# Sixteen more chunks of a decoder layer as seven products, with local attention, head and tail rearranged

## The chip, the cores and the metric

One core of one Trainium2 chip runs the whole layer. The metric is the device time of one execution in microseconds (us). Three runs of the kernel before gave a median of 2082.5 us (2082.36 to 2082.59).

## The reference

A decoder layer on 256 tokens of width 2048, all in float32. Every `w` is a weight in HBM; a mixer has eight channel groups that mix tokens (u, v) beside a sliding-window attention of 16 heads (q, k, v), and a cross-attention of four heads reads 256 rows of memory.

```python
h = x
h = h + 0.5 * swiglu(rmsnorm(h, g_ffn1), w1_gate, w1_up, w1_down)   # 2048 -> 5632 -> 2048
z = rmsnorm(h, g_mix) @ w_in                                        # u, v, q, and a narrow k, v
y_a = spatial_gating(z[..., :o_q], g_v, w_s, b_s)                   # gelu(u) * (w_s @ norm(gelu(v)) + b_s)
y_b = window_attention_sinks(q, k, v, sinks)
h = h + concat(rmsnorm(y_a), rmsnorm(y_b)) @ w_out
h = h + cross_attention(rmsnorm(h, g_x), rmsnorm(mem, g_mem), w_xq, w_xkv, w_xo)
h = h + 0.5 * swiglu(rmsnorm(h, g_ffn2), w2_gate, w2_up, w2_down)
return rmsnorm(h, g_final)
```

## The kernel before

**Numbers.** Float32 factors are split into a high part (a cast to the rounded type fp32r, L150, on ACT) and a low part (a subtraction, L151, on DVE). A product of two such factors is three passes on PE: high by high, high by low, low by high.

**Chunks.** The tokens stand as two blocks of 128. Weights come from HBM in chunks of 1 MB, [128, 4, 512]: four slots, two row groups by two column groups, which is a 2 x 2 block of a matrix (B11, B12, B21, B22). `load` (L303) issues the DMA on SP's queue, and splits the chunk into `wh` and `wl`; there are three `raw` buffers and two of `wh` and of `wl`. A chunk meets a *pair* of rows of the activations, also 2 x 2 (A11 to A22, with their own high and low parts). `Unit.multiply` (L354) multiplies it in one of three kinds:

- N and C: four sums of two products, 8 x 3 passes = 24 matmuls of 512 columns. C gathers them so that a later S chunk can add to the same banks.
- S: seven products instead of eight (Strassen's scheme, in Winograd's form), 7 x 3 = 21 matmuls. They need four sums of weight slots, `t` (L314, L317, L318, on DVE), split into `th` and `tl` (one buffer each), sums of rows of the pair (L198 to L208), and at the end of the unit sums of the seven results (`seven_early`, `seven_late`, L496 to L511).

A *unit* is a series of chunks that adds up in the same four to eight PSUM banks. Four banks are accumulators of the pool `acc`; four more, of the pool `trp`, hold the other results (P1, Q6, Q7, R) and everything small: transposes and attention.

**Stages.** In this order: f1g (11 units of 8 chunks, gate and up of the first FFN), f1d (22 pairs by two halves of w_down, in four units of 8, 15, 14 and 7 chunks), q, a narrow kv, v, u, mv and mk (values and keys of the memory), wo (out of the mixer), xq (memory queries, two units), xo, f2g, f2d. The kinds of a unit's chunks are written as a string. f1g and f2g have `KINDS` = "CCSCSCSC", mv1 and mk `KINDS_M`, the down stages `KINDS_D` (a kind for each of the 22 pairs), whose six S stand for 12 S chunks in each FFN. q, v, u, mv0 and xq are plain: `unit` (L446) with eight N chunks. Altogether 102 chunks are of kind S.

**Order.** PE runs in the order of the program (`PINNED`). The other engines' instructions are put in order by a scheduler. `push` loads a chunk and leaves its multiplication pending until the next `push` has issued its own load, so that DVE and ACT are one chunk ahead of PE. After every sixth matmul `side_step` runs a piece of side work (transposes, attention, normalization), except in chunks that the unit marks `alone`, and in a run of S chunks whose banks are the `trp` ones. `post` of a unit's last chunk reads its results, in high priority; `later` holds work that is done some pushes on.

**Head.** `prep1` and `plain_gu_unit` run the first f1g unit in kind N: 12 warm-up matmuls (L99) on a tile of ones, the first chunk's weights in four pieces, the transposed input xT in [128, 2, 256] blocks (the first on ACT's queue, L86), and from chunk 1 the blocks of x for `h`. Rows are scaled and split straight from xT (`split_scaled`), and the rows of other units are normalized and transposed beside it.

**Tail.** `ffn` for f2 adds to `h` (L537); `on_final` takes squares of each 512 columns (L140, ACT) and the product with the final gain (L1263). After the last matmul: `rstd_of` for both token blocks (a sum, a multiply-add, a power on POOL, L129 to L135), then the scaling by it (L1277, L1282, L1285) and the output DMAs.

**Local attention.** `attend` (L925) is a side generator. In each round it writes scores `sc`, takes the softmax, transposes the probabilities `pT`, and multiplies them by the values into `po`, one `trp` bank that it holds for all its rounds.

## Time and profile before

| what | kernel before |
|---|---|
| median of three runs | 2082.5 us |
| the profiled execution | 2082.59 us |
| its span in the profile | 2080.9 us |
| PE, matmuls in flight | 2065.4 us (99%), 9518 instructions |
| PE, weight loads | 1712.7 us (82%) |
| DVE busy | 1684.6 us (81%), 1621 instructions |
| ACT busy | 1137.1 us (55%), 1104 instructions |
| DMA | 402.16 MB, 193 GB/s on average |

The profiled execution's own time is 1.7 us longer than its span. Matmuls overlap, so that an instruction's duration (0.39 us for 512 columns) is longer than the distance to the next one's start. A DVE instruction's duration, too, reaches a little beyond the start of the next one.

### The profile page before, as it was taken

To read this page: it belongs to the slowest core of one execution; us is meant where nothing else is said; L and a number is where in the kernel's file an instruction comes from. 1 tells how busy PE (TensorE), PEld (TensorE's weight loads), DVE (VectorE), ACT (ScalarE), POOL (GpSimd) and SP (SyncE) were. 2 spreads that over 40 slices of the span, in tenths; PEclk is the share of its full clock that TensorE was granted. 3 is DMA by queue.
4 is the path that set the end of the run, shared out by engine and by line. 5 is a ranking of instruction groups with operands and counts; after the bars stand their busy time and mean duration, and the time that the engine had idled before them with its cause. 6 is when DMAs were issued, how large, how long until landed. Compare 5 with 4: busy or idle time off the path is not lost.

```text
span 2080.9 us, 23813 instructions
## 1 busy us (share of the span) xinstructions
PE 2065.4 (99%) x9518; PEld 1712.7 (82%) x9518; DVE 1684.6 (81%) x1621; ACT 1137.1 (55%) x1104; POOL 30.2 (1%) x51
## 2 busy tenths in 40 slices
PE   9999999999999999999999999999999999999998
PEld 7788888888888888888888888888888888888886
DVE  5988888888987845968888656798888888889877
ACT  7655555555544655555555455665555555555444
POOL 0000000000000000200000000000000000000000
PEclk9999999999999999999999999999999999999999
DMA  8555555555555564535555544455555555555563
GB/s 305 182 199 206 201 191 182 207 198 195 202 201 202 198 227 167 184 137 201 189 195 186 181 160 143 181 194 210 182 206 197 203 184 202 202 202 202 185 219 121
DMA packets 60111, 402.16 MB, mean 193 GB/s; under 512 B 6864, under 2 KB 8928, under 8 KB 12768
## 3 DMA queue, kind: packets, MB, share of 16 engines
q1 hardware_dynamic: 57280, 393.50, 52.7%
q0 software_dynamic: 2016, 6.30, 0.9%
q8 instruction: 74, 1.21, 0.2%
q10 hardware_dynamic: 704, 0.84, 0.1%
q14 instruction: 37, 0.30, 0.0%
HBM read 398.52 MB, written 2.10 MB: 193 GB/s over the span
## 4 chain that ended last, share of the span: by engine, by line
PE 97%; DVE 2%; ACT 1%; issue 0%; DMA 0%; POOLq 0%; POOL 0%; SPq 0%; DVEq 0%
PE f2gQ L368 16%; PE f1gQ L368 15%; PE f2dQ L368 6%; PE f1dQ L368 6%; PE f2gP L368 6%; PE f1gP L368 5%; PE f2dP L368 3%; PE f1dP L368 3%; PE woQ L368 2%; PE xoQ L368 2%; PE xqQ L368 2%; PE f2dR L368 2%; PE f1dR L368 2%; PE mk1Q L368 1%; PE mk0Q L368 1%; PE mv1Q L368 1%
## 5 line engine op out<-in xcount | busy, mean ns | idle before, releaser
L151 DVE TENSOR_TENSOR f1gwl<-f1gw,f1gwh 128x2048 fp32r<-128x2048 f32 (+1 forms) x91 | 185.7, 2042 | 55.8 <-ACT f1gwh L150 55.6
L150 ACT CAST f2gwh<-f2gw 128x1536 fp32r<-128x1536 f32 (+1 forms) x88 | 154.3, 1753 | 133.2 <-PE f2gQ L368 97.6
L150 ACT CAST f1gwh<-f1gw 128x2048 fp32r<-128x2048 f32 (+1 forms) x91 | 155.9, 1714 | 126.0 <-PE f1gQ L368 89.4
L151 DVE TENSOR_TENSOR f2gwl<-f2gw,f2gwh 128x1536 fp32r<-128x1536 f32 (+1 forms) x88 | 183.6, 2087 | 41.1 <-ACT f2gwh L150 40.9
L368 PE MATMUL f2gQ<-f2gwh,n4fh 128*128 128x512 f32 x363 | 141.4, 390 | 0.0
L368 PE MATMUL f2gQ<-f2gwh,n4fl 128*128 128x512 f32 x363 | 141.3, 389 | 0.0
L368 PE MATMUL f1gQ<-f1gwh,n1fh 128*128 128x512 f32 x330 | 128.8, 390 | 0.0
L368 PE MATMUL f1gQ<-f1gwh,n1fl 128*128 128x512 f32 x330 | 128.5, 389 | 0.0
L150 ACT CAST f1dwh<-f1dw 128x2048 fp32r<-128x2048 f32 (+1 forms) x44 | 79.1, 1797 | 84.5 <-PE f1dQ L368 65.3
L150 ACT CAST f2dwh<-f2dw 128x2048 fp32r<-128x2048 f32 (+1 forms) x44 | 79.1, 1797 | 83.3 <-PE f2dQ L368 67.8
L368 PE MATMUL f2gQ<-f2gwl,n4fh 128*128 128x512 f32 x363 | 115.7, 392 | 0.0
L151 DVE TENSOR_TENSOR f1dwl<-f1dw,f1dwh 128x2048 fp32r<-128x2048 f32 (+1 forms) x44 | 94.2, 2143 | 26.1 <-ACT f1dwh L150 23.5
L151 DVE TENSOR_TENSOR f2dwl<-f2dw,f2dwh 128x2048 fp32r<-128x2048 f32 (+1 forms) x44 | 94.2, 2143 | 22.8 <-ACT f2dwh L150 20.0
L368 PE MATMUL f1gQ<-f1gwl,n1fh 128*128 128x512 f32 x330 | 105.1, 392 | 0.0
L151 DVE TENSOR_TENSOR f2gtl<-f2gt,f2gth 128x2048 fp32r<-128x2048 f32 x33 | 75.6, 2291 | 17.9 <-ACT f2gth L150 17.4
L151 DVE TENSOR_TENSOR f1gtl<-f1gt,f1gth 128x2048 fp32r<-128x2048 f32 x30 | 68.7, 2291 | 16.7 <-ACT f1gth L150 16.2
L368 PEld LDWEIGHTS f2gQ<-f2gwh,n4fl 128*128 128x128 f32 x363 | 68.1, 188 | 14.2
L368 PEld LDWEIGHTS f2gQ<-f2gwh,n4fh 128*128 128x128 f32 x363 | 68.2, 188 | 14.1
L368 PEld LDWEIGHTS f2gQ<-f2gwl,n4fh 128*128 128x128 f32 x363 | 67.3, 188 | 13.5
L150 ACT CAST f2gth<-f2gt 128x2048 fp32r<-128x2048 f32 x33 | 63.1, 1912 | 24.8 <-DVE f2gt L318 20.0
L368 PEld LDWEIGHTS f1gQ<-f1gwh,n1fl 128*128 128x128 f32 x330 | 62.0, 188 | 12.8
L368 PEld LDWEIGHTS f1gQ<-f1gwh,n1fh 128*128 128x128 f32 x330 | 62.0, 188 | 12.8
(700 smaller groups left out, 5714.7 us busy)
## 6 DMA issues: line engine op xcount, KB each, us to landing
f2gw<-in_w_gu SPq DMA_DIRECT2D x88, 1024.0 KB, 4.8
f1gw<-in_w_gu SPq DMA_DIRECT2D x87, 1024.0 KB, 4.8
f1dw<-in_w_down SPq DMA_DIRECT2D x44, 1024.0 KB, 4.8
f2dw<-in_w_down SPq DMA_DIRECT2D x44, 1024.0 KB, 4.8
wow<-in_w_out SPq DMA_DIRECT2D x16, 1024.0 KB, 4.8
xqw<-in_w_xq SPq DMA_DIRECT2D x16, 1024.0 KB, 4.8
xow<-in_w_xo SPq DMA_DIRECT2D x16, 1024.0 KB, 4.8
qw<-in_w_in SPq DMA_DIRECT2D x8, 1024.0 KB, 4.9
```

The source lines that it names most:

```text
L150: nc.scalar.copy(hi, src)
L151: nc.vector.tensor_tensor(lo, src, hi.bitcast(F32), ALU.subtract)
L368: nc.tensor.matmul(self.banks[name], x, y, start=name not in self.begun, stop=self.left[name] == 0)
```

## The change

Seven edits in one.

1. **Kinds.** q, v and the two xq units go from `unit` to `seven_unit`, with "CCCSCCSC". The rows of n2 and n3, which q, v, u and xq read, get these kinds as well, so that the S pairs are sums of rows, and their scale is applied to the results from an estimate of the row's scale that is corrected later, as in the other mixed units. `KINDS_D` gets two more S.
2. **Results by SBUF.** Those units have `dst=None`: results go to SBUF tiles `at`, and the activations of q, v and xq read them there.
3. **Halves.** `th` and `tl` are two tiles of [128, 2, 512] each, cast and subtracted one after the other.
4. **Local attention** holds `po` for a round: ACT copies 64 columns a head to `yb`, and the division by the sums is done there. `seven_unit` doesn't wait any more until all attention is done.
5. **Small moves.** v's squares are `later` work and its scaling goes from chunk 2 to chunk 4 of u; u runs chunks 0 and 7 alone, v chunk 7; `seven_early` runs after the last S chunk.
6. **Head.** 8 warm-up matmuls; the first xT rows in [128, 256] pieces on SP's queue, ahead of and between the pieces of the weights; chunk 1 in pieces too; the blocks of x one chunk later, and the squares and normalization of the first rows later as well.
7. **Tail.** The last two down chunks are kept and multiplied together (`multiply_two`), first all of token block 0, then all of block 1; `finished(tb)` scales and stores a block as soon as its sums are there. The mean of the first three quarters of the squares (`known`) is worked out earlier.

```diff
-WARM = 12
+WARM = 8
...
-            split(th, tl, t)
-            for i, name in enumerate(("T1", "T3", "T2", "T4")):
-                b[name] = th[:, i, :], tl[:, i, :]
+            for i, names in enumerate((("T1", "T3"), ("T2", "T4"))):
+                th, tl = [
+                    stream.tile([P, 2, 512], F32R, tag=f"{n}{i}", name=nm(s + n), bufs=1)
+                    for n in ("th", "tl")
+                ]
+                split(th, tl, t[:, 2 * i:2 * i + 2, :])
+                for j, name in enumerate(names):
+                    b[name] = th[:, j, :], tl[:, j, :]
...
+        def multiply_two(self, first, second, between):
+            steps = [self.passes("N", p, b, True)[0] for p, b in (first, second)]
+            half = len(steps[0]) // 2
+            for tb in range(TB):
+                for k in range(tb * half, (tb + 1) * half, half // 2):
+                    for s in steps:
+                        self.run(s[k:k + half // 2])
+                between(tb)
...
+    KINDS_MIX = "CCCSCCSC"
+    KINDS_X = "CCCSCCSC"
...
-    KINDS_D = "NNNNSNSN" + "NNSNSNN" + "NNSNSNN"
+    KINDS_D = "NNSNSNSN" + "NSNSNSN" + "NNSNSNN"
...
-    def seven_unit(s, w, cb, pairs, dst, late=None):
-        u = Unit(s, KINDS_M, sparse=True)
-        until(lambda: len(attended) == 2 * TB)
+    def seven_unit(s, kinds, w, cb, pairs, dst, late=None, beside=None, alone=()):
+        u = Unit(s, kinds, alone=alone, sparse=True)
...
+            if dst is None:
+                at = {(0, 0): got["p1"], (1, 1): s2(s), (0, 1): got["v"], (1, 0): got["z"]}
+                seven_late(u, got, lambda tb, j: at[tb, j])
+                late(at)
+                return
...
-    unit("q", w_in, 2, n2, late_q, beside_queries)
+    seven_unit("q", KINDS_MIX, w_in, 2, n2, None, late_q, beside_queries)
...
-            po = bank("wop")
...
+                po = bank("wop")[:, :per * 64].rearrange("p (a d) -> p a d", a=per)
...
+                nc.scalar.copy(ybh[:, hs, :], po)
+                yield 1
...
-    unit("v", w_in, 1, n2, late_v)
+    seven_unit("v", KINDS_MIX, w_in, 1, n2, None, late_v, alone=(7,))
...
+    def finished(tb):
+        ms = tiny.tile([P, 1], F32, tag="ms", name=nm("ms"))
+        nc.vector.tensor_scalar(
+            ms, summed[tb][-1], 1.0 / D, known[tb], op0=ALU.mult, op1=ALU.add
+        )
...
+        nc.scalar.activation(last[:, at:], last[:, at:], AF.Copy, scale=rs)
+        nc.scalar.dma_start(out[rows_, 1024 + at:], last[:, at:])
+        nc.vector.tensor_scalar_mul(first, first, rs)
+        nc.sync.dma_start(out[rows_, :1024], first)
```

By the programs' orders, PE has 48 matmuls of 512 columns fewer (8478 for 8526) and 4 warm-ups fewer, DVE 264 instructions more and ACT 202 more.

DVE in the first down unit, from the low half of its third chunk on (f1dw a weight chunk, f1dwl its low half, f1dt its sums and f1dtl their low half, f1af and f1afl a pair's rows); before:

```order
L151 TENSOR_TENSOR f1dwl_618_3604<-f1dw_616_3602,f1dwh_617_3603 128x2048
L151 TENSOR_TENSOR f1afl_620_3609<-f1a_215_1207,f1afh_619_3608 128x512
L151 TENSOR_TENSOR f1afl_628_3656<-f1a_262_1498,f1afh_627_3655 128x512
L151 TENSOR_TENSOR f1afl_630_3658<-f1af_631_3659,f1afh_629_3657 128x512
L314 TENSOR_TENSOR f1dt_635_3695<-f1dw_632_3691 128x1024
L151 TENSOR_TENSOR f1dwl_626_3651<-f1dw_624_3649,f1dwh_625_3650 128x2048
L317 TENSOR_TENSOR f1dt_635_3695<-f1dt_635_3695,f1dw_632_3691 128x512
L151 TENSOR_TENSOR f1afl_642_3736<-f1a_262_1498,f1afh_641_3735 128x512
L318 TENSOR_TENSOR f1dt_635_3695<-f1dt_635_3695,f1dw_632_3691 128x512
L151 TENSOR_TENSOR f1afl_667_3879<-f1a_309_1789,f1afh_666_3878 128x512
L151 TENSOR_TENSOR f1afl_677_3922<-f1a_309_1789,f1afh_676_3921 128x512
L151 TENSOR_TENSOR f1dwl_634_3693<-f1dw_632_3691,f1dwh_633_3692 128x1536
```

and after, from the low half of the second chunk on:

```order
L147 TENSOR_TENSOR f1dwl_668_3691<-f1dw_666_3689,f1dwh_667_3690 128x2048
L203 TENSOR_TENSOR f1af_673_3699<-f1a_227_1237,f1af_673_3699 128x128
L308 TENSOR_TENSOR f1dt_681_3739<-f1dt_681_3739,f1dw_678_3735 128x512
L204 TENSOR_TENSOR f1af_673_3699<-f1a_227_1237,f1af_673_3699 128x128
L309 TENSOR_TENSOR f1dt_681_3739<-f1dt_681_3739,f1dw_678_3735 128x512
L147 TENSOR_TENSOR f1dwl_680_3737<-f1dw_678_3735,f1dwh_679_3736 128x1536
L147 TENSOR_TENSOR f1afl_672_3698<-f1af_673_3699,f1afh_671_3697 128x512
L147 TENSOR_TENSOR f1dtl_683_3746<-f1dt_681_3739,f1dth_682_3745 128x1024
L147 TENSOR_TENSOR f1dtl_685_3750<-f1dt_681_3739,f1dth_684_3749 128x1024
L147 TENSOR_TENSOR f1dwl_690_3791<-f1dw_688_3789,f1dwh_689_3790 128x2048
L147 TENSOR_TENSOR f1afl_692_3796<-f1a_227_1237,f1afh_691_3795 128x512
L305 TENSOR_TENSOR f1dt_701_3829<-f1dw_698_3825 128x1024
```

Before, the third chunk is plain and the next S chunk is the fifth; now the third chunk has its sums and both its subtractions of 1024, and the sums of the next S chunk begin two rows later.

ACT at the end of q and the start of kv (qs the scaled q rows, kvwh the high half of a kv chunk, qT the transposed q); before:

```order
L150 CAST qwh_957_5498<-qw_956_5497 128x2048
L150 CAST kvwh_963_5534<-kvw_962_5533 128x2048
L844 ACTIVATE qs_898_5195<-qP2_912_5249,rs_938_5365 128x512
L844 ACTIVATE qs_898_5195<-qQ3_913_5250,rs_938_5365 128x512
L844 ACTIVATE qs_899_5196<-qR_914_5251,rs_938_5365 128x512
L150 CAST kvwh_968_5572<-kvw_967_5571 128x2048
L844 ACTIVATE qs_899_5196<-qQ4_915_5252,rs_938_5365 128x512
L862 COPY qT_972_5579<-qTp_976_5604 128x512
```

and after:

```order
L146 CAST kvwh_1120_5859<-kvw_1119_5858 128x2048
L136 ACTIVATE junk_1122_5864,parts_1022_5456<-mr_1113_5825 128x512
L898 ACTIVATE qs_1023_5457<-qp1_1115_5850,rs_1084_5675 128x512
L136 ACTIVATE junk_1123_5866,parts_1022_5456<-mr_1114_5827 128x512
L898 ACTIVATE qs_1024_5458<-q_1124_5892,rs_1084_5675 128x512
L146 CAST kvwh_1126_5903<-kvw_1125_5902 128x2048
L898 ACTIVATE qs_1023_5457<-qv_1116_5851,rs_1084_5675 128x512
L898 ACTIVATE qs_1024_5458<-qz_1117_5852,rs_1084_5675 128x512
L916 COPY qT_1130_5910<-qTp_1134_5935 128x512
```

Before, one activation of qs stands behind the second cast of kv, and reads a PSUM bank; now two do, and all four read SBUF tiles (qp1, q, qv and qz).

DVE at the very end (hg the rows times the final gain, ms and partsf of the mean square); before:

```order
L129 TENSOR_REDUCE ss_2661_15199<-partsf_1805_10220 128x1
L1263 TENSOR_TENSOR hg_1810_10225<-h_119,gf_1804_10218 128x512
L537 SCALAR_TENSOR_TENSOR h_119<-f2dQ4_2628_14962,h_119 128x512
L133 TENSOR_SCALAR ms_2662_15201<-ss_2661_15199 128x1
L1263 TENSOR_TENSOR hg_1810_10225<-h_119,gf_1804_10218 128x512
L1282 TENSOR_SCALAR hg_1808_10223<-hg_1808_10223,rs_2663_15203 128x512
L129 TENSOR_REDUCE ss_2664_15205<-partsf_1806_10221 128x1
L133 TENSOR_SCALAR ms_2665_15207<-ss_2664_15205 128x1
L1277 TENSOR_SCALAR hg_1807_10222<-hg_1807_10222,rs_2663_15203 128x1024
L1277 TENSOR_SCALAR hg_1809_10224<-hg_1809_10224,rs_2666_15209 128x1024
L1282 TENSOR_SCALAR hg_1810_10225<-hg_1810_10225,rs_2666_15209 128x512
```

and after:

```order
L568 SCALAR_TENSOR_TENSOR h_113<-f2dR_3009_15761,h_113 128x512
L1334 TENSOR_SCALAR ms_3045_15979<-partsf_2075_10794,known_2081_10800 128x1
L1327 TENSOR_TENSOR hg_2080_10799<-h_113,gf_2074_10792 128x512
L1347 TENSOR_SCALAR hg_2077_10796<-hg_2077_10796,rs_3046_15981 128x1024
L1320 TENSOR_TENSOR known_2082_10801<-known_2082_10801,partsf_2076_10795 128x1
L1321 TENSOR_SCALAR known_2082_10801<-known_2082_10801 128x1
L568 SCALAR_TENSOR_TENSOR h_113<-f2dQ4_3010_15762,h_113 128x512
L1327 TENSOR_TENSOR hg_2080_10799<-h_113,gf_2074_10792 128x512
L1334 TENSOR_SCALAR ms_3049_16021<-partsf_2076_10795,known_2082_10801 128x1
L1347 TENSOR_SCALAR hg_2079_10798<-hg_2079_10798,rs_3050_16023 128x1024
L1350 TENSOR_SCALAR hg_2080_10799<-hg_2080_10799,rs_3050_16023 128x512
```

The two blocks' steps were interleaved, with both scalings of 1024 at the end; now block 0's mean and scaling (hg_2077) stand ahead of the last sum from PSUM (Q4).

## Rows read from the trace of the kernel before

**Rows 1.** The page: the span, each engine's busy time, its share and its instructions, and the share of each engine in the chain that ended last.

```profile
span 2080.9 us, 23813 instructions
PE 2065.4 (99%) x9518; PEld 1712.7 (82%) x9518; DVE 1684.6 (81%) x1621; ACT 1137.1 (55%) x1104; POOL 30.2 (1%) x51
...
PE 97%; DVE 2%; ACT 1%; issue 0%; DMA 0%; POOLq 0%; POOL 0%; SPq 0%; DVEq 0%
```

**Rows 2.** What PE waits for, nine groups: line, the engine, tile and line that released it; us in total, times, longest. The first and the last.

```profile
PE warm L99 <- DVE ones L90: 1.1, 1, 1.1
...
PE f1gP L368 <- DVE n0l L145: 0.2, 1, 0.2
```

**Rows 3.** The chain in order of time, one of its 1876 pieces, in the last chunk of f1g: start, us, what.

```profile
479.26 4.08 PE f1gQ L368 x18
```

**Rows 4.** Busy time by stretches, core 0: the first down stage, u and the second down stage. Columns: from:to, us; busy us (instructions) of PE, PEld, DVE, ACT and POOL; granted PE clock, DMA share, GB/s.

```profile
482.00:718.00 236.00, 235.38 (x1049) 194.38 (x1049) 202.24 (x194) 124.33 (x107) 1.14 (x2) 1.00 0.56 198
...
830.00:888.00 58.00, 58.00 (x284) 47.54 (x283) 49.25 (x86) 35.37 (x57) 10.95 (x15) 1.00 0.54 190
...
1840.00:2070.00 230.00, 230.00 (x1021) 190.48 (x1020) 198.09 (x187) 117.95 (x98) 0.00 (x0) 1.00 0.52 183
```

**Rows 5.** Timeline of DVE in f1g, where it runs without a break: start, us, engine, line, operation, out<-in.

```profile
57.29 1.22 DVE L314 TENSOR_TENSOR f1gt<-f1gw 128x1024 f32<-128x1024 f32 x1
58.43 2.29 DVE L151 TENSOR_TENSOR f1gwl<-f1gw,f1gwh 128x2048 fp32r<-128x2048 f32 x1
60.63 0.42 DVE L202 TENSOR_TENSOR n1f<-n1r 128x256 f32<-128x256 f32 x1
60.96 0.69 DVE L151 TENSOR_TENSOR n1fl<-n1r,n1fh 128x512 fp32r<-128x512 f32 x1
...
66.13 0.68 DVE L318 TENSOR_TENSOR f1gt<-f1gt,f1gw 128x512 f32<-128x512 f32 x1
66.73 1.75 DVE L151 TENSOR_TENSOR f1gwl<-f1gw,f1gwh 128x1536 fp32r<-128x1536 f32 x1
68.40 0.68 DVE L151 TENSOR_TENSOR n1fl<-n1f,n1fh 128x512 fp32r<-128x512 f32 x1
```

**Rows 6.** Busy time by stretches, the first two units (23 chunks) of each down stage. Columns as above.

```profile
483.30:604.40 121.10, 121.10 (x540) 100.27 (x539) 105.09 (x105) 65.07 (x53) 0.00 (x0) 1.00 0.55 193
1845.00:1966.00 121.00, 121.00 (x539) 100.20 (x539) 105.28 (x101) 63.64 (x52) 0.00 (x0) 1.00 0.56 198
```

**Rows 7.** Timeline in the first down unit: DVE's low half of a chunk, and PE's first matmuls that read it.

```profile
485.14 2.29 DVE L151 TENSOR_TENSOR f1dwl<-f1dw,f1dwh 128x2048 fp32r<-128x2048 f32 x1
...
492.25 0.62 PE L368 MATMUL f1dP<-f1dwl,f1afh 128*128 128x512 f32 x2
```

**Rows 8.** What DVE and ACT wait for in the down stages. Columns as in the list of PE's waits.

```profile
DVE f1dwl L151 <- ACT f1dwh L150: 23.5, 22, 3.8
DVE f2dwl L151 <- ACT f2dwh L150: 20.0, 19, 3.8
...
DVE f2dtl L151 <- ACT f2dth L150: 6.8, 6, 2.1
DVE f1dtl L151 <- ACT f1dth L150: 6.3, 7, 2.1
...
ACT f1dwh L150 <- PE f1dQ L368: 65.3, 26, 6.2
```

**Rows 9.** Timeline from q to kv: ACT's second cast of kv, its last scaling of q, and PE's first transposes of q.

```profile
763.70 1.91 ACT L150 CAST kvwh<-kvw 128x2048 fp32r<-128x2048 f32 x1 [0.44 <-PE qQ L368]
765.51 0.68 ACT L844 ACTIVATE qs<-qQ,rs 128x512 f32<-128x512 f32 x1
...
765.88 0.91 PE L858 MATMUL qTp<-ident,qs 128*128 128x128 f32 x4
```

**Rows 10.** Timeline of the head: the first scaled rows of x on ACT, and matmuls of the first chunk.

```profile
6.18 0.51 ACT L144 ACTIVATE n0h<-n0r,sm 128x256 fp32r<-128x256 f32 x1 [0.84 <-DMA n0r<-in_xT]
...
6.74 0.50 PE L368 MATMUL f1gP<-f1gwh,n0h 128*128 128x512 f32 x1 [0.41 <-ACT n0h L144]
...
9.09 0.63 PE L368 MATMUL f1gP<-f1gwh,n0l 128*128 128x512 f32 x1 [0.22 <-DVE n0l L145]
...
9.94 0.63 PE L368 MATMUL f1gQ<-f1gwh,n0h 128*128 128x512 f32 x1
10.37 0.63 PE L368 MATMUL f1gQ<-f1gwh,n0l 128*128 128x512 f32 x1
```

**Rows 11.** Busy time by stretches in the head. Columns as above; the granted clock is the third from the end.

```profile
10.00:12.00 2.00, 2.00 (x6) 1.60 (x5) 0.59 (x2) 0.35 (x2) 0.00 (x0) 0.50 0.98 380
12.00:14.00 2.00, 2.00 (x9) 1.57 (x8) 0.37 (x1) 2.00 (x3) 0.00 (x0) 0.82 1.06 392
```

**Rows 12.** Timeline of the tail: the last matmul, the end of block 1's last square, its power on POOL, and the issue of the last output.

```profile
2070.18 0.39 PE L368 MATMUL f2dQ<-f2dwl,f2afh 128*128 128x512 f32 x1
...
2071.87 0.19 ACT L140 ACTIVATION_READ_ACCUMULATOR junk<-h 128x1 f32 x1
...
2073.36 0.93 POOL L135 TENSOR_TENSOR rs<-ms,mhalf 128x1 f32<-128x1 f32 x1 [0.92 <-DVE ms L133]
...
2075.53 0.48 SPq L1283 DMA_DIRECT2D out<-hg  x1
```

**Rows 13.** Busy time in the stretch in which the output is written. Columns as above.

```profile
2073.50:2079.50 6.00, 0.00 (x0) 0.00 (x0) 1.52 (x3) 0.72 (x1) 0.78 (x1) 0.57 0.92 350
```

More of the change, by code (lines that the diff above doesn't have):

```diff
@@ L301, in layer_kernel, with load @@
     }
-    def load(s, w, kind, pieces):
+    def load(s, w, kind, pieces, between):
         raw = stream.tile([P, 4, 512], F32, tag="raw", name=nm(s + "w"), bufs=3)
@@ L365, in multiply, with run @@
                     last.append((name, ah, bl))
-            for n, (name, x, y) in enumerate(steps + behind):
+            return steps, behind
+        def run(self, steps):
+            for n, (name, x, y) in enumerate(steps):
                 self.left[name] -= 1
@@ L430, in turn, with push @@
         later[:] = [(n - 1, f) for n, f in later if n]
-    def push(u, i, w, p, post=None, pieces=None, beside=None):
-        b = load(u.s, w, u.kinds[i], pieces)
+    def push(u, i, w, p, post=None, pieces=None, beside=None, before=None, ending=None):
+        if before is not None and i:
+            before(i)
+        b = load(u.s, w, u.kinds[i], pieces, lambda n: before(i, n) if i == 0 else None)
         if beside is not None:
@@ L442, in run @@
             tight[0] = u.sparse and first <= i <= last
-            u.multiply(u.kinds[i], p(), b, i in (0, len(u.kinds) - 1))
+            if ending is None:
+                u.multiply(u.kinds[i], p(), b, i in (0, len(u.kinds) - 1))
+            elif not u.kept:
+                u.kept.append((p(), b))
+            else:
+                u.multiply_two(u.kept[0], (p(), b), ending)
             held[0] = False
@@ L448, in layer_kernel, with unit @@
     BLOCKS = (("P2", 0, 0), ("Q3", 0, 1), ("R", 1, 1), ("Q4", 1, 0))
-    def unit(s, w, cb, pairs, late, beside=None):
-        u = Unit(s, "N" * 8)
+    def unit(s, w, cb, pairs, late, beside=None, alone=()):
+        u = Unit(s, "N" * 8, alone=alone)
         for i in range(8):
@@ L562, in early, with late @@
                 later.append((0, rest))
-        def late(u):
+        def late(u, blocks=range(TB)):
             for name, tb, j in BLOCKS:
-                add(hb(tb, j), u[name], tb, j)
-                if on_block is not None:
-                    on_block(j0 + j, tb)
+                if tb in blocks:
+                    add(hb(tb, j), u[name], tb, j)
+                    if on_block is not None:
+                        on_block(j0 + j, tb)
         return early, late
@@ L582, in added_unit, with ffn @@
             )
-    def ffn(s, get, rs, wgu, wd, on_block, first=None):
+    def ffn(s, get, rs, wgu, wd, on_block, first=None, on_token_block=None):
         acts = [None] * 22
@@ L642, in plain_gu_unit @@
         def plain_gu_unit(c):
-            pairs_, prep, rs0 = first
+            pairs_, before, prep, rs0 = first
             u = Unit(s + "g", "N" * 8, alone=(7,))
@@ L766, in layer_kernel, with first_pairs @@
     quad = []
-    ahead = [raw0]
-    def prep1(i):
-        if i % 2 == 0:
+    ahead = []
+    def first_pairs(i, piece=None):
+        if i % 2 == 0 and not piece:
             quad[:] = [
@@ L773, in prep1 @@
             ]
-        raw = ahead.pop()
+        if not piece:
+            n0.append(Pair("n0", "N", [t[:, i % 2] for t in quad]))
+            if piece is not None:
+                ahead.append(s2("n0r").rearrange("p (k t) -> p k t", k=2))
+        for k in range(2) if piece is None else (piece,) if piece < 2 else ():
+            if piece is not None:
+                nc.sync.dma_start(ahead[0][:, k, :], xT[k * P:(k + 1) * P, :])
+            row_loaded(n0[i], ahead[0], i, k, G_FFN1)
+        if piece in (None, 1):
+            ahead.pop()
+    def prep1(i):
         if i < 7:
```

156 lines of the change are left out of this document (80 added, 76 removed).

## The prediction

> **What bounds the kernel now.** I read the page first, for the engines' shares. PE has matmuls in flight for 2065.4 us of a span of 2080.9, DVE works for 1684.6 and ACT for 1137.1, and the chain that ended last is 97% PE, 2% DVE and 1% ACT [rows 1]. A busy share alone would not settle it, since matmuls overlap. So the second view was what PE waits for: nine groups, from 1.1 us at the warm-up down to 0.2, 4.8 us in all [rows 2]. The third was the chain in order of time: 18 matmuls of 512 columns take 4.08 us, 226.8 ns for each, one behind another [rows 3]. A chunk of four products (24 matmuls) is then 5.44 us of PE and one of seven products (21) is 4.76. The fourth view was each stage by itself: PE fills 235.38 of 236 us of the first down stage and all of u and of the second down stage, at full granted clock, while DVE fills 85 or 86% of the same time [rows 4]. Hence two rules for the sum: a matmul left out is 0.227 us off the end, and work of DVE or ACT costs nothing until its engine runs out of time within a stage. Only the first 15 us and the last 10 are not PE-bound.
>
> The sum is made against the profiled execution, 2082.6 us: its span of 2080.9 and 1.7 around it. The median of the runs is 2082.5, so nothing is to be converted.
>
> **The change part by part.** *Fewer matmuls.* q and v get two seven-product chunks each, the two xq units two each, and two more down pairs are read by two halves of the weights in each of two FFNs: 2 + 2 + 4 + 8 = 16 chunks. Each saves three matmuls: 48 x 0.2268 = **-10.9 us**, all of it on the path by [rows 2, 3]. What pays for it is DVE. By the distances from start to start, 1024 elements take 1.14 us, 2048 take 2.20, 512 take 0.60 and 1536 take 1.67 [rows 5]. A plain chunk is one subtraction of 2048 (2.20). A seven-product chunk is 1.14 + 0.60 + 0.60 + 1.67 for the sums and the first subtraction, and 2 x 1.14 for the halved second: 6.29, so 4.09 more. A pair that is kept for seven products costs 1.33 more (a second subtraction of 512, 0.60; one sum of 256 at 0.33 by the same rows, and two of 128 at an estimated 0.2).
>
> *The down stages are where this could be too much.* Their first two units hold 23 chunks, and three of the four new seven-product chunks of a stage fall in them. There DVE is busy for 105.1 of 121.1 us in the first FFN and 105.3 of 121 in the second [rows 6]. To this come 3 x 4.09 for the chunks, 2 x 1.33 for the pairs and 9 x 0.08 for the halving (2 x 1.14 against 2.20): 15.7, so 120.8, and 121.0 in the second. PE in turn drops by nine matmuls to 119.1 and 119.0. DVE's bare work is 1.7 and 2.0 us longer than PE's. Against that stands its lead: it ends a low half at 487.43 and PE first reads it at 492.25, 4.8 us later [rows 7]. For it to go wrong stand DVE's waits on ACT's casts: 23.5 + 6.3 us in the first down stage and 20.0 + 6.8 in the second [rows 8], so some 29.8 x 23/44 = 15.6 in the first's 23 chunks. They should shrink: ACT itself mostly waits until PE has let go of a buffer, as an engine does that runs ahead, and an engine that is late finds its casts done. With no wait left the lead covers the excess: 0. With a quarter left, it is 1.85 + 3.9 - 4.8 = 0.95 for each stage. I take that quarter, as the nearer to the row on the lead: **+1.9** for both, between 0 and 4 for the plain case; half and all are a rival below.
>
> *The halved casts and subtractions* cost DVE 0.08 us a chunk by the distances (118 x 0.08 = 9 us over the whole kernel), hidden wherever DVE has room; in the two tight stretches they are in the sum already, and in return PE can start on the first half 1.1 us earlier. The Trainium skill, VectorE: DVE Perf Modes, section "The TRN2 errata", says that a fixed latency is paid once by a large tile and per tile by small ones. It would set it at 157 ns a chunk (estimate from its formula, (N + 151) cycles at 0.96 GHz), which agrees with the durations of single instructions but not with the distances, where half of that is overlapped; 9 x 0.08 = 0.7 us more DVE work in each tight stretch, and 0.7 us later there if nothing covered it.
>
> *q to kv.* The q rows of the last two products are no longer read from the banks but from SBUF, and two such activations instead of one stand on ACT behind the second kv cast. Today PE's first q transposes start at 765.88, right after that cast and while the last activation (0.68 us) runs, and fill 0.91 us with a short wait [rows 9]. One more activation ahead of them is **+0.7** (0, if the scheduler's order is hidden by kv matmuls that stand ahead; 2.0, if the whole cast is in front).
>
> *v, u, xq, local attention.* In these stages DVE is at 85% at most (u), and u gets no new chunks, only the v scaling later; the new sums stand in the others. A bank held only for a round frees nothing that PE waits for today. The deferred squares stand on ACT. **+0.5** (0 to 3), no row shows such a wait.
>
> *Head.* The first product starts at 6.74, since the rows of x are ready only at 6.18. It then takes until 9.09 for PE to be fed without a break, and after that thin stretch the granted clock falls: matmuls stand 0.43 apart from 9.5 to 12.5 [rows 10], 0.50 of full clock from 10 to 12 us and 0.82 from 12 to 14 [rows 11]. That is 1.2 against 2.4 GHz. The change issues the first 128 rows of x ahead of the weights, on SP, and keeps the loads of h out of the way for one chunk. I count 0.5 for the earlier start and 1.4 for the cold stretch (seven distances of 0.43 against 0.227): **-1.9**. The bounds are 0, if the thin stretch remains and the clock falls all the same (four warm-up matmuls fewer, ending about 1.7 us earlier, speak for that), and -3.0, if nothing of the thin stretch is left.
>
> *Tail.* The last matmul starts at 2070.18; the sums for the last token block wait behind the first block's on DVE and POOL (its square is there at 2072.06, its power runs only at 2073.36), the last output is issued at 2075.53 [rows 12], and between 2073.5 and 2079.5 the DMA moves 2.1 MB at 350 GB/s [rows 13]. The change runs the last two chunks by token block, so that block 0's sums are complete 24 matmuls before the end; its mean stands on DVE behind R's sum (12 matmuls before the end), so half of the output leaves about the time of the last matmul, and the second power follows its own square at once. The chain gains 1.1 us (2073.36 against 2072.2), and the transfer left is 1 MB, 3.0 us instead of 6, most of which the chain hides: -1.8. Against it stands a new need: PE reads the last chunk's low half 8 matmuls after the third-last chunk (kind S) ends, 1.8 us, and not 24 and 2. That chunk takes over the buffers of this S chunk, which lets go of its high half 12 matmuls (2.7 us) before its end; then come a cast of 1.9 us and a subtraction of 2.3 (durations in [rows 5, 9]), done 1.5 after the S chunk's end. The margin is 0.3 us. I take a wait of 0.3, so **-1.5**, between -2.4 (no wait) and +1.8 (the chain alone, -0.6, and a wait of 2.4, if the cast comes only at the S chunk's end).
>
> Sum: 2082.6 - 10.9 + 1.9 + 0.7 + 0.5 - 1.9 - 1.5 = **2071.4 us**.
>
> **The rivals.** (a) *DVE becomes the bound in the down stages*, because its waits on ACT's casts survive. For: 120.8 us of bare work against 119.1, and 29.8 and 26.8 us of waits [rows 6, 8]. Against: the lead, and that PE waits for DVE nowhere there today [rows 2]. With half of the waits left, a stage is late by 1.85 + 7.8 - 4.8 = 4.85 and the whole gives 2071.4 - 1.9 + 9.7 = 2079.2. With all left, 12.65 each: 2094.8, slower than before. It decides from 8.6 us per stage, that is when 11.5 of the 15.6 us of waits survive.
> (b) *PE's matmul count is not the limit*, and the 48 matmuls give nothing back: 2071.4 + 10.9 = 2082.3. Weight loads fill 82% and DVE 81% of the span [rows 1], so that another pace could set the chunks. Against it: distances of 226.8 ns in chunks of either kind and no waits. The Trainium skill, Perfetto Trace Analysis, section "Identifying the Most-Contended Engine", says that matmul busy time misjudges TensorE and that the weight loads' share is the better measure; by that rule PE and DVE would be about equally loaded. The trace bears out the warning on overlap, yet not the conclusion.
> (c) *Everything fits*: no new wait, head and tail at their better ends: 2082.6 - 10.9 - 3.0 - 2.4 = 2066.3.
>
> **How the numbers follow.** The forecast with a quarter of the waits or less, and with the bounds of the small terms, 2066 to 2077: chance 0.76. This takes in (c) down to 2066; below it, 0.04. Half of the waits, about 2079: 0.12, half of it to either side of 2078. All of them, 2095: 0.05. (b), 2082: 0.03. The range 2066 to 2078 holds 0.76 + 0.06 = 0.82. A measurement of this kernel can tell about 0.2% (4.2 us) from no change: faster is under 2078.3 and slower over 2086.7. Faster: 0.76 + 0.04 + 0.06 = 0.86; same: 0.06 + 0.03 = 0.09; slower: 0.05.
>
> **What would show it right or wrong.** PE's matmul groups add up to 48 fewer, and the distances in a chunk stay at 226.8 ns; if they grow, (b) has something. In the list of PE's waits, f1d and f2d low halves (wl, tl) by DVE show under 2 us for each stage; 5 or more is (a), and DVE's waits on f1dwh and f1dth then still stand at half of today's. A wait of PE on qs near kv is under 1 us. The granted clock between 9 and 14 us is at 1.00, or the head term is off. From the last matmul to the end it is about 8.5 us instead of 10.3. What would make the whole wrong is a wait that PE has in no place today, first in u, in the last three chunks of the second down stage, and in the seven-product units of xq, where results now pass through SBUF.

## The result and the profile after

| | before | changed |
|---|---|---|
| median | 2082.43 us (2082.12 to 2082.59, 4 runs) | 2071.91 us (2071.58 to 2072.54, 4 runs) |
| ratio, 95% interval | | 0.995 (0.9938 to 0.9962) |
| profiled execution, its span | 2082.59, 2080.9 us | 2071.58, 2069.9 us |

The change is 10.5 us (0.5%) faster; 2071.4 was forecast. Page of the changed kernel, against [rows 1]: span, busy times, chain.

```profile
span 2069.9 us, 24359 instructions
...
PE 2053.2 (99%) x9462; PEld 1699.0 (82%) x9462; DVE 1782.4 (86%) x1885; ACT 1196.8 (58%) x1307; POOL 36.0 (2%) x53
...
PE 96%; DMA 1%; DVE 1%; ACT 1%; issue 0%; SPq 0%; POOL 0%; POOLq 0%; DVEq 0%; ACTq 0%
```

DVE works 97.8 us more in a shorter span and PE is still the chain. What PE waits for now (all nine groups of the list, against [rows 2]; us in total, times, longest):

```profile
PE woQ L386 <- ACT n3r L234: 1.5, 1, 1.5
PE f1gP L386 <- ACT f1gwh L146: 1.3, 2, 1.1
PE xoQ L386 <- ACT n4r L234: 1.2, 1, 1.2
PE warm L97 <- DVE ones L88: 1.1, 1, 1.1
PE qTp L912 <- ACT qs L898: 0.8, 1, 0.8
PE xoP L386 <- ACT xofh L146: 0.7, 1, 0.7
PE f1gQ L386 <- DVE n1fl L147: 0.6, 1, 0.6
PE f2gP L386 <- DVE f2gwl L147: 0.3, 1, 0.3
PE xoP L386 <- DVE xofl L147: 0.2, 1, 0.2
```

Two things are to be seen. The down stages, where rival (a) put the danger, have no wait at all. And wo and xo, of which the prediction named neither, have two new ones (woQ, xoQ) of 2.7 us together. (New are also the one on qs, which was forecast, and one of 0.6 on n1fl, the low half of rows in f1g.) Busy time by stretches of the first down stage, against [rows 6] (columns as there): 119.1 us from PE's first matmul of the stage on, which is what the matmuls of its first two units take, and the first unit.

```profile
480.96:600.06 119.10, 119.10 (x530) 98.50 (x529) 116.64 (x126) 70.45 (x65) 0.00 (x0) 1.00 0.55 195
...
483.00:524.00 41.00, 41.00 (x186) 33.91 (x186) 40.70 (x46) 24.13 (x25) 0.00 (x0) 1.00 0.58 205
```

In the first unit DVE is busy for 40.70 of 41 us and PE is not held up. DVE's waits on ACT's casts over the whole of each stage, against [rows 8], fell from 23.5 + 6.3 to 11.1 in the first and from 20.0 + 6.8 to 10.0 in the second:

```profile
DVE f1dwl L147 <- ACT f1dwh L146: 11.1, 10, 3.0
DVE f2dwl L147 <- ACT f2dwh L146: 10.0, 9, 3.0
```

Against [rows 7], the lead, timeline in the first unit: the second low half of a chunk's sums, and PE's four matmuls that read the low halves. DVE is done at 514.45, 2.7 us ahead of the first of them; by the program's order the first two read the first half, so that the second half's own lead is two distances longer, some 3.1 us (before, a chunk's low half had 4.8).

```profile
513.23 1.22 DVE L147 TENSOR_TENSOR f1dtl<-f1dt,f1dth 128x1024 fp32r<-128x1024 f32 x1
...
517.13 1.07 PE L386 MATMUL f1dQ<-f1dtl,f1afh 128*128 128x512 f32 x4
```

Against [rows 12], the tail: last matmul, POOL's second power, issue of the last output. From the last matmul's end (2061.09) to the end of the span it is 8.8 us; it was 10.3.

```profile
2060.70 0.39 PE L386 MATMUL f2dQ<-f2dwl,f2afh 128*128 128x512 f32 x1
...
2062.96 0.55 POOL L1338 TENSOR_TENSOR rs<-ms,mhalf 128x1 f32<-128x1 f32 x1 [2.73 <-DVE ms L1334]
...
2064.73 0.44 SPq L1351 DMA_DIRECT2D out<-hg  x1
```

### The profile page after: what moved, and what is told of

Same layout as the page of the kernel before. It is cut to its first block, busy times and chain, and to the rows that moved or that the text cites. A ratio compares the mean times of both kernels' runs of the same rounds, so it can differ in the third digit from the quotient of the medians.

```text
span 2069.9 us, 24359 instructions
## 1 busy us (share of the span) xinstructions
PE 2053.2 (99%) x9462; PEld 1699.0 (82%) x9462; DVE 1782.4 (86%) x1885; ACT 1196.8 (58%) x1307; POOL 36.0 (2%) x53
## 4 chain that ended last, share of the span: by engine, by line
PE 96%; DMA 1%; DVE 1%; ACT 1%; issue 0%; SPq 0%; POOL 0%; POOLq 0%; DVEq 0%; ACTq 0%
PE f1gQ L386 15%; PE f2gQ L386 15%; PE f1dQ L386 6%; PE f2dQ L386 6%; PE f1gP L386 6%; PE f2gP L386 5%; PE xqQ L386 3%; PE f1dP L386 3%; PE f2dP L386 3%; PE woQ L386 2%; PE xoQ L386 2%; PE f1dR L386 2%; PE f2dR L386 2%; PE vQ L386 2%; PE qQ L386 2%; PE mk1Q L386 1%
## 5 line engine op out<-in xcount | busy, mean ns | idle before, releaser
L147 DVE TENSOR_TENSOR f1gwl<-f1gw,f1gwh 128x1536 fp32r<-128x1536 f32 (+2 forms) x94 | 186.0, 1982 | 59.5 <-ACT f1gwh L146 59.1
L146 ACT CAST f1gwh<-f1gw 128x1536 fp32r<-128x1536 f32 (+2 forms) x94 | 156.5, 1665 | 131.1 <-PE f1gQ L386 68.1
L147 DVE TENSOR_TENSOR f1dwl<-f1dw,f1dwh 128x2048 fp32r<-128x2048 f32 (+1 forms) x44 | 92.0, 2092 | 11.2 <-ACT f1dwh L146 11.1
L147 DVE TENSOR_TENSOR f2gtl<-f2gt,f2gth 128x1024 fp32r<-128x1024 f32 x66 | 78.6, 1217 | 0.0
L386 PEld LDWEIGHTS f2gQ<-f2gwl,n4fh 128*128 128x128 f32 x363 | 67.3, 188 | 13.6
L146 ACT CAST f2gth<-f2gt 128x1024 fp32r<-128x1024 f32 x66 | 67.4, 1047 | 15.7 <-DVE f2gt L305 15.2
L147 DVE TENSOR_TENSOR f1gtl<-f1gt,f1gth 128x1024 fp32r<-128x1024 f32 x60 | 71.6, 1217 | 0.0
```

The costliest lines, as they stand in the source:

```text
L146: nc.scalar.copy(hi, src)
L147: nc.vector.tensor_tensor(lo, src, hi.bitcast(F32), ALU.subtract)
L386: nc.tensor.matmul(self.banks[name], x, y, start=name not in self.begun, stop=self.left[name] == 0)
```

## The experiments

All twelve are the changed kernel with one edit or two. Times vary by chip by a few tenths, so the last column compares each with the kernel before on the same chip; the changed kernel itself stands at -10.5.

| run | edit | median us (lowest to highest) | ratio to before (95%) | against before |
|---|---|---|---|---|
| e1_down_old | old kinds of the down pairs | 2076.94 (2075.86 to 2077.78) | 0.9974 (0.9963 to 0.9985) | -5.2 |
| e2_whole | th and tl whole | 2086.03 (2085.42 to 2087.93) | 1.0019 (1.001 to 1.0028) | +3.9 |
| e3_head_old | old head | 2070.99 (2070.90 to 2071.71) | 0.9946 (0.9934 to 0.9959) | -11.2 |
| e4_tail_last | both blocks finished at the end | 2072.59 (2072.32 to 2073.06) | 0.9953 (0.994 to 0.9967) | -9.6 |
| e5_ops_halved | one tile, halved instructions | 2071.80 (2070.81 to 2072.24) | 0.9949 (0.9935 to 0.9963) | -10.4 |
| e6_whole_down_old | e1 and e2 together | 2075.81 (2075.30 to 2076.91) | 0.997 (0.9959 to 0.9982) | -6.4 |
| e7_o_alone | no side work ahead of S in wo, xo | 2072.90 (2072.80 to 2073.54) | 0.9956 (0.9944 to 0.9969) | -9.3 |
| e8_down_four | one more S pair | 2082.34 (2081.03 to 2083.66) | 1.0 (0.9991 to 1.0009) | +0.1 |
| e9_o_whole | whole in wo and xo alone | 2069.21 (2068.12 to 2070.32) | 0.9936 (0.9923 to 0.9948) | -13.3 |
| e10_o_whole_head_old | e9 and the old head | 2068.35 (2068.25 to 2068.57) | 0.9933 (0.9919 to 0.9946) | -14.1 |
| e11_o_whole_warm12 | e9 and 12 warm-ups | 2067.73 (2067.60 to 2068.31) | 0.993 (0.9917 to 0.9942) | -14.7 |
| e12_mix_one | one S in q, v, xq | 2075.55 (2075.28 to 2075.86) | 0.9967 (0.9954 to 0.9979) | -6.9 |

The intervals of e3, e9, e10 and e11 overlap with each other, and those of all runs but e1, e2 and e8 with the changed kernel's (0.9938 to 0.9962). Differences of a few us rest on the medians, and on the lengths of stages in the traces.

**e1_down_old.** What do matmuls cost in the down stages, and does DVE take part of it back?

```diff
-    KINDS_D = "NNSNSNSN" + "NSNSNSN" + "NNSNSNN"
+    KINDS_D = "NNNNSNSN" + "NNSNSNN" + "NNSNSNN"
```

> The changed kernel with the old kinds of the down pairs (8 seven-product chunks fewer, 24 matmuls more). If PE's matmuls set the time in the down stages and DVE's extra work there is covered by its lead: 24 x 0.2268 = 5.4 us slower than the changed kernel, 2077.3. If DVE is already the bound there (rival a) and gives back part of the gain: only 0 to 3 us slower, 2072 to 2075. If matmuls do not set the pace (rival b): no difference.

It is 5.3 us slower than the changed kernel (-5.2 against -10.5). From the first matmul of the stage to the next stage's, f1d grew by 2.63, and f2d, to its last matmul, by 2.74; 12 matmuls each are 2.72. So the 24 matmuls cost their full price, and DVE took nothing back.

**e2_whole.** What is the halving of th and tl worth?

```diff
-                split(th, tl, t[:, 2 * i:2 * i + 2, :])
+            split(th, tl, t)
```

> The changed kernel with th and tl whole again: one cast and one subtraction of 2048 instead of two of 1024. If the halves only add overhead to a DVE with room: no difference within 0.5 us (2071.9). If they are what keeps PE fed in the tight down units, where a second low half is ready only about 3 us before it is read: the first half would come 1.1 us later, and waits of PE on f1dtl and f2dtl appear, 1 to 4 us in all (2073 to 2076). If the halved ACT casts cause the new waits of PE on n3r and n4r in wo and xo (2.7 us): 1 to 3 us faster.

The second expectation had the place right and the size far too small: 14.4 us slower, and slower than the kernel before. f1d is 7.35 and f2d 8.27 us longer, wo and xo 1.59 and 1.48 shorter. The head of the list of PE's waits, and DVE's waits on casts in f1d:

```profile
PE f2dQ L383 <- DVE f2dtl L147: 4.6, 7, 0.8
PE f1dQ L383 <- DVE f1dtl L147: 3.8, 6, 0.8
...
DVE f1dwl L147 <- ACT f1dwh L146: 14.3, 17, 2.2
...
DVE f1dtl L147 <- ACT f1dth L146: 3.5, 6, 0.9
```

In the timeline of one such wait (start, us, engine, line, operation) the chain is ACT's, then DVE's:

```profile
512.93 1.92 ACT L146 CAST f1dwh<-f1dw 128x2048 fp32r<-128x2048 f32 x1 [4.04 <-PE f1dQ L383]
...
514.74 1.91 ACT L146 CAST f1dth<-f1dt 128x2048 fp32r<-128x2048 f32 x1
514.88 2.29 DVE L147 TENSOR_TENSOR f1dwl<-f1dw,f1dwh 128x2048 fp32r<-128x2048 f32 x1 [0.31 <-ACT f1dwh L146]
...
517.08 2.28 DVE L147 TENSOR_TENSOR f1dtl<-f1dt,f1dth 128x2048 fp32r<-128x2048 f32 x1
...
519.42 1.20 PE L383 MATMUL f1dQ<-f1dtl,f1afh 128*128 128x512 f32 x4 [0.61 <-DVE f1dtl L147]
```

The cast of the sums stands on ACT behind the next chunk's cast, which waits 4.04 us for PE to let go of a buffer; on DVE the low half of the sums then stands behind the next chunk's. PE gets it at 519.42, as DVE ends it. In the changed kernel the halves of the sums stand on ACT ahead of the next chunk's cast, and DVE ends the second low one at 514.45, 4.9 us earlier (of this 1.1 is the stage's earlier start):

```profile
511.69 1.06 ACT L146 CAST f1dth<-f1dt 128x1024 fp32r<-128x1024 f32 x1 [2.77 <-PE f1dQ L386]
512.64 1.92 ACT L146 CAST f1dwh<-f1dw 128x2048 fp32r<-128x2048 f32 x1
```

The waits shown make up 8.4 of the 15.6 us. The distances of the matmuls place most of the rest: at these 13 waits they are longer by 10.5 us in all (0.99 us where 0.227 is usual, of which the list shows 0.61), and at the first two reads of f1dth and f2dth and the second of f1dtl and f2dtl, in pauses of some 0.1 us that the list leaves out, by 4.3 more; 14.8 in all.

**e5_ops_halved.** Is it the smaller instructions, or the two buffers?

```diff
-                    stream.tile([P, 2, 512], F32R, tag=f"{n}{i}", name=nm(s + n), bufs=1)
-                split(th, tl, t[:, 2 * i:2 * i + 2, :])
+            th = stream.tile([P, 4, 512], F32R, tag="th", name=nm(s + "th"), bufs=1)
+            tl = stream.tile([P, 4, 512], F32R, tag="tl", name=nm(s + "tl"), bufs=1)
+                two = slice(2 * i, 2 * i + 2)
+                split(th[:, two, :], tl[:, two, :], t[:, two, :])
```

> The changed kernel with th and tl as one tile of 2048 each, but still cast and subtracted in two halves. The whole ones cost 14 us against the changed kernel, 15.6 of it in the down stages. If the size of the instructions is what counts (a half is ready 1.1 us earlier, and the order of ACT and DVE follows): within 1 us of the changed kernel, 2071 to 2073. If it is that each half is a buffer of its own, free as soon as its own products are read: 2080 to 2086, with waits of PE on f1dtl and f2dtl. The waits of PE in wo and xo (2.7 us, gone with whole tiles) then stay in the first case and go in the second.

-10.4 against -10.5: as the changed kernel, with the waits in wo and xo as there. It is the size of the instructions, with the order that follows from it, and not the buffers.

**e6_whole_down_old.** Do whole tiles hurt where DVE isn't short? (The edits of e1 and e2.)

> The changed kernel with whole th and tl and the old kinds of the down pairs: q, v, xq, head and tail of the change alone. If whole tiles only hurt where DVE is short, which the old down stages are not: 24 matmuls more than the changed kernel (5.4 us) and the waits in wo and xo gone (3.1), so 2074.2. If whole tiles hurt anyhow: 2080 or more.

4.1 us slower than the changed kernel, 2.3 expected. The stages named are as expected: f1d +2.63, f2d +2.74, wo -1.60, xo -1.47, and no wait of PE in the down stages. But whole tiles also bring waits in f1g and f2g, here and in e2, and in no trace with halves:

```profile
PE f1gQ L383 <- DVE f1sg L639: 0.7, 1, 0.7
...
PE f2gQ L383 <- DVE f2gtl L147: 0.3, 1, 0.3
```

With a like one on f2gth, f2g is 0.96 longer than in e1, which has halves. With the 0.7 this is nearly the difference to what was expected. So the 15 us of e2 need both, whole tiles and the new down pairs; elsewhere whole tiles cost about one us a stage (f1g, f2g) or gain 1.5 (wo, xo).

**e8_down_four.** How far is DVE from being the bound?

```diff
-    KINDS_D = "NNSNSNSN" + "NSNSNSN" + "NNSNSNN"
+    KINDS_D = "NSNSNSNS" + "NSNSNSN" + "NNSNSNN"
```

> The changed kernel with one more seven-product pair in the first down span (NSNSNSNS): 4 chunks and 12 matmuls more saved, 2.7 us. In the first unit DVE is already busy for 40.7 of 41.0 us. If its lead still covers that: 2069.2. If the first two units now run at DVE's pace (5.4 us more work in each unit, PE 0.7 less, a lead of about 2.6): PE waits on f1dwl, f1dtl, f2dwl and f2dtl, 3 us or more in each stage, and the kernel is slower than the changed one: 2073 to 2080.

10.6 us slower than the changed kernel, though PE has 12 matmuls fewer. f1d is 4.86 longer and f2d 6.29. Waits of PE, and busy time of the second unit and of a stretch of f2d:

```profile
PE f1dQ L386 <- DVE f1dtl L147: 4.4, 3, 3.4
PE f2dQ L386 <- DVE f2dtl L147: 3.6, 2, 3.4
```

```profile
522.00:605.00 83.00, 78.83 (x349) 63.89 (x348) 82.73 (x90) 46.66 (x44) 0.00 (x0) 1.00 0.55 198
...
1880.00:1887.00 7.00, 5.83 (x16) 4.67 (x17) 7.00 (x9) 0.31 (x1) 0.00 (x0) 0.51 0.16 66
```

DVE is busy for 82.73 of 83 us and PE stands still for 4.17. One pair more, and DVE is the bound, as in rival (a), but by its own work: its waits on f1dwh are 8.5 us, less than the 11.1 of the changed kernel. Part of f2d's 6.29 is the clock: after PE's wait of 3.4 us, which ended at 1881.17, the granted clock is 0.51 up to 1887 and matmuls stand 0.43 us apart. After a like wait in f1d, which ended at 526.54, it stayed at 1.00.

**e7_o_alone and e9_o_whole.** Where do the new waits in wo and xo come from, and can they go?

```diff
-        u = Unit(s, kinds, LATE_O)
+        u = Unit(s, kinds, LATE_O, alone=(kinds.index("S") - 1,))   # e7
...
+            n = 4 if s in ("wo", "xo") else 2                       # e9, on e5
+            for i in range(0, 4, n):
+                split(th[:, i:i + n, :], tl[:, i:i + n, :], t[:, i:i + n, :])
```

> The changed kernel with no side work in the chunk ahead of the first seven-product chunk of each wo and xo unit, so that no transposed rows of n3 or n4 stand in the four banks that this chunk needs. If the waits of PE on n3r and n4r come from transposes whose copy stands on ACT behind a cast that itself waits for PE: both gone, 2.7 to 3.1 us faster, 2069.0. If the moved transposes are late for the next unit: waits on n3 and n4 rows in xq and f2g take the place, within 1 us of 2071.9.

> The changed kernel with whole casts and subtractions of th and tl in wo and xo alone, halves everywhere else. If the halves' place in ACT's order is what makes PE wait for n3r and n4r there, and their use is in the down stages alone: 3.07 us faster than the changed kernel (the two stages of the run with whole tiles), 2068.8. If the wait only moves on to f2g, as when the side work was moved: 2070 to 2071.

Timeline of the changed kernel at the wait in wo (start, us, engine, line, operation [idle before, releaser]): PE turns rows of n3 into a bank, ACT's copy of them (n3r) stands behind a cast of weights, and that waits for PE.

```profile
1128.21 0.60 PE L216 MATMUL n<-ident,n3s 128*128 128x128 f32 x4
...
1132.08 1.48 ACT L146 CAST wowh<-wow 128x1536 fp32r<-128x1536 f32 x1 [0.52 <-PE woQ L386]
...
1133.76 0.83 ACT L234 ACTIVATE n3r<-n,sm 128x256 f32<-128x256 f32 x2
...
1134.65 0.50 PE L386 MATMUL woQ<-woth,yafh 128*128 128x512 f32 x1 [1.48 <-ACT n3r L234]
```

The S chunk wants all four banks. e7 takes the transposes away from there: wo and xo become 1.77 and 1.49 us shorter, but f2g 3.35 longer, with these two in the list of waits, and 0.8 on f2gwh:

```profile
PE f2gQ L386 <- ACT n4r L234: 1.5, 1, 1.5
PE f2gP L386 <- DVE f2gwl L147: 1.2, 1, 1.2
```

So the wait moved, as the second expectation had it. In e9 wo and xo are 1.60 and 1.49 shorter, neither wait is left, and nothing takes their place: 2.8 us faster than the changed kernel (3.07 expected). With e6 and e2 this shows that the halves made these waits. By the timeline it is their order on ACT: in e9 the same copy stands ahead of the cast.

```profile
1132.54 0.83 ACT L234 ACTIVATE n3r<-n,sm 128x256 f32<-128x256 f32 x2
1133.26 1.48 ACT L146 CAST wowh<-wow 128x1536 fp32r<-128x1536 f32 x1
```

**e3_head_old, e10, e11.** What is the new head worth?

```diff
+WARM = 12                                             # e3, e10, e11
...
+    nc.scalar.dma_start(raw0, xT[:T, :]...)           # e3, e10: the old loads, pieces and places
```

> The changed kernel with the head of the kernel before: 12 warm-up matmuls, the first rows of x in one block on ACT's queue, pieces only in chunk 0, the old places of the loads of h and of the squares. If the head is worth what the end of chunk 0 shows (12.58 us against 15.38): 2.8 us slower, 2074.7. If the later normalization gives part of it back in f1g (a wait of 0.6 us on n1fl stands there now): 2.0 to 2.4 slower.

> The same with the head of the kernel before as well. If the new head is worth nothing or slightly less than that (0.9 us slower on the changed kernel): 2067.9 to 2068.8, with a spread under 1 us. If the earlier difference was chance, and the head brings what its end of chunk 0 shows: 2070 to 2071.5.

> As the run with whole wo and xo and the new head, with 12 warm-up matmuls for 8. If the new head loses in some executions because PE stands still between the end of the warm-up (4.9 us) and the first product (6.0), and the granted clock falls after it: about 1 us faster than with 8 and a smaller spread, 2067.8. If the arrival of the weights sets the pace up to 30 us: no difference, 2068.8, and the spread stays.

By medians the old head is 0.7 us faster on the changed kernel (each against the kernel before on its own chip) and 0.9 on e9 (on one chip). The spreads are 0.8 and 0.3 us against 1.0 and 2.2, so that this isn't shown to be more than chance. In both traces with the old head 0.24 us of it lies in the tail, which the edit doesn't touch; that stays open. The new head with 12 warm-ups is the fastest: 1.5 better than with 8, spread 0.7, and 0.6 better than the old head. The profiled execution of the changed kernel shows its head at full pace: warm-up, first product, first product of the next chunk.

```profile
1.12 3.78 PE L97 MATMUL warm<-ones 128*128 128x128 f32 x16 [1.12 <-DVE ones L88]
6.04 0.50 PE L386 MATMUL f1gP<-f1gwh,n0h 128*128 128x512 f32 x1 [1.14 <-ACT f1gwh L146]
...
12.58 0.39 PE L386 MATMUL f1gP<-f1gwh,n0h 128*128 128x512 f32 x1
```

That was not the usual case. Of the ten traces with this head and 8 warm-ups seven have 4 to 11 matmuls at a distance of 0.43 us. e9 is one, in the timeline:

```profile
5.73 0.80 PE L385 MATMUL f1gP<-f1gwh,n0h 128*128 128x512 f32 x1 [0.82 <-ACT f1gwh L146]
6.32 0.63 PE L385 MATMUL f1gP<-f1gwh,n0l 128*128 128x512 f32 x1
6.75 0.63 PE L385 MATMUL f1gP<-f1gwl,n0h 128*128 128x512 f32 x1
```

There PE had stood still from 4.90, where the warm-up ended, to 5.73. By the clock's record in the traces there are two cases. In five of the seven (e4, e7, e8, e9, e12) the granted clock had not risen when the warm-up ended: the record begins at 9.55 to 13.07 us, with 1.00, and there the distances fall to 0.227. In e2 and e5 it rose at 4.0 and 4.9 and was at 0.50 again from 7.4 to 10.8 and from 8.3 to 11.7. With 12 warm-ups it rose in all four traces between 4.6 and 6.6, before the first product, and e3, e10 and e11 have no such distances; in the kernel before, also with 12, it fell again, and there are eight [rows 10, 11].

How much of these 2 to 3 us reaches the end depends on the weights. ACT's cast of chunk 3 of the first unit in the changed kernel, and busy time from 4 to 30 us:

```profile
22.05 1.91 ACT L146 CAST f1gwh<-f1gw 128x2048 fp32r<-128x2048 f32 x1 [3.17 <-DMA f1gw<-in_w_gu]
```

```profile
4.00:30.00 26.00, 24.54 (x102) 18.21 (x100) 13.93 (x21) 16.40 (x27) 0.00 (x0) 1.00 1.01 377
```

The cast waits 3.17 us for its chunk, and the DMA engines are full until 30 us (share 1.01). With the new head chunk 4 starts at 29.9 us at the earliest, with the old at 31.5. A start of chunk 1 at 12.5 instead of 13.6 brings nothing: in e1 chunk 4 starts at 31.0, in e9 at 29.9. A later one counts in full, since from there PE needs 16.3 us for three chunks: in e7 and e8, with 11 and 10 slow distances, chunk 1 starts at 15.3 and 15.5 and chunk 4 at 31.6 and 31.8. With the old head the slow stretch is nearly free: chunk 4 starts at 31.70 in the kernel before, which has it, and at 31.46 and 31.49 in e3 and e10, which have not.

The new head also has a price of its own. PE's wait on n1fl, 0.6 us at 68 us (in the list of the changed kernel), stands in all eleven traces with it and in none of the three with the old one: the first rows' squares and normalization come later. The first matmul of f1d has all of this behind it. It starts at 481.5 us in e3 and e10, at 480.8 to 482.6 in the ten traces with the new head and 8 warm-ups, and at 480.9 in e11.

**e4_tail_last.** Which part of the tail's gain is the order by token block?

```diff
-    ffn("f2", ..., on_final, on_token_block=finished)
+    ffn("f2", ..., on_final)
     flush()
+    for tb in range(TB):
+        finished(tb)
```

> The changed kernel with its last two down chunks one after the other and both token blocks finished after the last matmul (the new formula for the mean and the new split of the scaling stay). If running them by token block is what brings the 1.5 us of the tail: 1.5 us slower, 2073.4. If the shorter chain of the mean brings most of it: under 0.8 slower. If the two chunks together cost a wait that this hides: faster.

0.9 us slower. From the last matmul to the end it is 9.64 us, against 8.78 in the changed kernel and 10.31 in the kernel before: 0.86 of the 1.53 us are the order, the other 0.67 the shorter chain and the new split of the scaling, which weren't taken apart.

**e12_mix_one.** Do matmuls set the time in q, v and xq too?

```diff
-    KINDS_MIX = "CCCSCCSC"
-    KINDS_X = "CCCSCCSC"
+    KINDS_MIX = "CCCCCCSC"
+    KINDS_X = "CCCCCCSC"
```

> The changed kernel with one seven-product chunk for two in q, v and both xq units (12 matmuls more). If PE sets the time in these stages: 2.7 us slower than the changed kernel, 2074.6. If DVE or ACT is the limit in one of them: less, down to 2072.

3.6 us slower, 2.7 expected. By stages: q +0.67 (three matmuls are 0.68), v and u together +0.67, xq +1.80 (1.36 expected). So no limit of DVE or ACT hides there. The rest lies in f1g and f1d, which the edit doesn't touch.

## Why the prediction was right, and where it was not

The time was right by half a microsecond. The largest term carries that; the closeness is luck, since the errors of the smaller terms, 2 us and more each, cancel.

**Fewer matmuls, -10.9.** Right. e1 and e12 give matmuls back at 0.22 to 0.30 us each. Rival (b) is out.

**Down stages, +1.9.** Measured 0: no wait, and e1 finds the full 5.4 us. Two sizes were off here, and they cancel. The bare work was put too high: DVE is busy for 116.6 us in the 119.1 in which 120.8 was worked out (the pieces of that were not measured). And the waits on ACT's casts shrank only to 11.1 of 29.8 over the stage, 37% where a quarter was taken. That DVE's time sets the stage once it has no room left was right: e8 shows it by more work. In e2 17.8 us of the first stage's waits survive, and there the rival's own formula gives 1.85 + 17.8 x 23/44 - 4.8 = 6.4 us; measured 7.35.

**The halves.** Here the step itself failed. They were put down as 9 us of DVE time with no effect, "and in return PE can start on the first half 1.1 us earlier", as an aside. They are what makes the change possible: without them the down stages are 15.6 us longer and rival (a) comes true, between its two cases: 2086.0. They also bring the waits in wo and xo. The Trainium skill (VectorE: DVE Perf Modes, section "The TRN2 errata") says that small tiles each pay a fixed latency, and the traces agree (two of 1.22 us for one of 2.28); by it the halves would only cost. The order in the queues repaid that with 14.4 us.

**q to kv, +0.7.** Right: the transposes of q in kv take 0.70 us longer, with a wait of 0.8 on qs.

**v, u, xq, +0.5 (0 to 3).** The size was off and the place missing: 2.7 us of waits in wo and xo. The prediction looked at the stages whose kinds change and not at those that turn their rows beside them, and did not ask which casts the halves would change places with. In v, u and mv0 there was no wait of PE.

**Head, -1.9 (0 to -3.0).** Wrong in size; in sign it isn't settled. At the first matmul of f1d the profiled execution is 0.5 us ahead of e3 with the old head, the other traces lie between 0.7 ahead and 1.1 behind, and by medians the old head is 0.7 to 0.9 us faster. Three steps of it failed. The cold stretch was counted at 1.4 us, but at chunk 4 it had cost the kernel before 0.2, since the weights arrive no earlier. Four warm-ups fewer, which the lower bound held against the change, cost 1.5 us by medians (e11): in most traces the clock was low in the first chunk, and the sign that was named, 1.00 between 9 and 14 us, holds for the profiled execution and not for these. And the later normalization, which brought the wait of 0.6 on n1fl, was in no term.

**Tail, -1.5.** Right in sum: 10.3 to 8.8. No wait for the last chunk came (0.3 was taken), and the rest gained 1.5 (1.8 was taken).

Put together by stages, from the two profiled executions (2080.9 to 2069.9, 11.0 less): matmuls -10.9, q to kv +0.7, wo and xo +2.8, tail -1.5, as said above; head and f1g together -2.2, f1d another -1.0, f2g -0.3, and v to mk +1.5 beyond their matmuls. Of the -2.2, 1.7 are there with the old head as well (e3): PE no longer waits or hesitates at f1gth and f1gtl, 1.3 by the distances, and the slow stretch is gone, 0.2 at chunk 4. In f1d a wait of 0.5 on n2fl is gone, half of the -1.0. In f2g the waits on f2gth and f2gtl are gone (0.7), and one of 0.3 on f2gwl came in this execution. The 1.5 us of v to mk stay open: attention runs at other places there, and no wait shows.

The fastest kernel here, e11 (whole casts in wo and xo, new head, 12 warm-ups), is 14.7 us below the kernel before.

## What to carry to other kernels

Where an engine ahead of the bottleneck is near 100% busy, look at what stands in its queues in front of the tile that is read next: cutting one instruction in two added a little work and took 14 us off the time, by the timelines because a cast that waits for a buffer no longer stood ahead of one that PE needed. The same cut made new waits in two other stages; it is worth making only in the stages that need it. A gain at the start of a kernel counts only if what is late next (here the transfers up to 30 us) moves as well. And one trace of a start is not enough: ten of the same head differed by 1.9 us at the end of f1g.
